# GpSimd's share of layer 0 and of the LayerNorms moved to VectorE and ScalarE or folded away, in a two-layer float32 encoder

## The chip, the cores and the metric

The kernel runs on one core of one Trainium2 chip. The metric is the device time of one execution in microseconds, as the median of three timed executions. Beside these stands one execution taken with the hardware profiler; all rows and durations in this text come from that one.

## The reference, cut to what matters

Two encoder layers over 256 tokens with 2048 features, all in float32. `cond` is silu(c); `g`, `sc` and `sh` are columns of the modulation.

```
for l in range(2):
    mod = cond @ w_ada[l] + b_ada[l]               # 6 parts: sh1, sc1, g1, sh2, sc2, g2
    u = x * (1.0 + sc1) + sh1
    proj = u @ w_in[l]                             # queries, keys, values of three groups of heads
    ... three attentions (4, 6 and 6 heads), each RMS-normalised -> y
    x = layer_norm(ALPHA * x + (1.0 + g1) * (y @ w_o[l]), ln1_g[l], ln1_b[l])
    u = x * (1.0 + sc2) + sh2
    gu = u @ w_gu[l]
    h = silu(gu[..., :5632]) * gu[..., 5632:]
    x = layer_norm(ALPHA * x + (1.0 + g2) * (h @ w_down[l]), ln2_g[l], ln2_b[l])
```

ALPHA is the square root of 2, and `layer_norm` divides by the root of the variance plus 1e-5.

## The kernel before, in words

**Layout.** Features lie on the 128 partitions, the 256 tokens on the free axis. A tile of 128 features by 256 tokens is one k of a product; a product of depth 2048 has 16 of them. The residual state is `ax`, 16 such tiles.

**Products.** TensorE multiplies in a reduced float32 form, so each operand is split into two halves that are exact in it: a weight piece `raw` (128x2048, 1 MB, one DMA on SP's queue) becomes `hi` on ScalarE (L246) and `lo` = raw - hi on VectorE (L247), each in two pieces of 1024 columns. An input tile X holds its high half in columns 0 to 255 and its low half in 256 to 511. For one 128x128 block of weights, a pair of matmuls runs: `hi` against all 512 columns (L262, or L538 in a stream), and `lo` against the first 256 (L263, L539). The accumulator has two halves that still have to be added: `combine` copies the second half on ScalarE (`cmb`, L279) and adds the first on VectorE (L282); `combine_add`, for a sum that is continued, uses ScalarE (L286), GpSimd (L287) and VectorE (L288). Only the last product of a run, `gemm_last` (L273), uses three matmuls of 256 columns for a block and one 256-column accumulator.

**Buffers.** `raw` and the modulation's weights `ada` share four buffers of 1 MB, in the order in which they are asked for on SP; `hi` and `lo` have four buffers each. A DMA therefore waits on SP until the fourth piece before it has been used up by VectorE.

**Modulation.** A column of 128 features is one VectorE pass over 128x2048 of `w_ada` (L200), 96 for a layer, followed by `ada_finish`, which adds the bias, and 1.0 for scales and gates (L190): in layer 0 once for each column. `first_x` makes the first 16 input tiles out of scale and shift (parts 1 and 0) as they arrive. The other columns are spread over the products by `pace` and `need`. DEFER = 6 columns of parts 4 and 3 are left for the first feed-forward.

**GpSimd.** It scales `ax` by ALPHA (L386), sums squares for the RMS norms (L328), adds in `combine_add` and in `residual` (L509, L518), and in `ln_and_next` computes coefficients (L461 to L463) and the new `ax` = ALPHA * (normalised * g + b) for every k (L493). In the head of a product that follows a LayerNorm it also makes the second `lo` piece of every weight tile but the first.

**Heads.** After a LayerNorm the next product starts with six tiles of n side by side, so that each X that arrives feeds six pairs. For each k VectorE makes `lt` from `ax` (L479, L480), ScalarE makes `lu` (L491) and the high half of X (L291), VectorE the low half of X (L292). There are three such heads: the first feed-forward (`gu0`, twelve tiles of which the first 11 k are summed while the last X arrive, results `gup`), the second layer's w_in (`in1`) and its feed-forward (`gu1`).

**Order.** Within an engine instructions run in the order in which a scheduler put them, with priorities from the order of the code; `ada` passes of the first two parts of layer 0 have high priority, all others low.

## Time and profile before

| | |
|---|---|
| three timed executions | 2382.51, 2383.88, 2376.82 us; median 2382.51 us |
| profiled execution, by its span | 2378.3 us, 4.2 us under the median of the timed ones |
| mean granted TensorE clock | 0.980 of full speed |
| busy: TensorE, VectorE, ScalarE, GpSimd | 94%, 76%, 50%, 19% of the span |
| moved by DMA | 590.62 MB, 248 GB/s on average |

The stages by time: 0 to 167 us first modulation columns and first part of w_in; 167 to 373.6 us attention of layer 0 with the rest of w_in; 373.6 to 460 us w_o of layer 0; to 466 us its LayerNorm; 466 to 554 us head of the first feed-forward (to the end of the sums over 11 k); to 1250 us the rest of it and the second LayerNorm; 1250 to 1302 us head of w_in of layer 1; to 1600 us its attention and w_o; 1600 to 1650 us LayerNorm and head of the second feed-forward; the rest to the end. The busy share of TensorE counts matmuls that wait inside for data, so lost time is read against the pitch of undisturbed matmuls and from waits, stage by stage.

### The profile page before, as it was taken

The numbers are of one execution on the slowest core, as the hardware profiler recorded it, in microseconds if no ns is written. First come the engines' busy times: TensorE is split into PE (matmuls) and PEld (weight loads), VectorE is DVE, ScalarE is ACT, GpSimd is POOL, SyncE is SP. The second block draws the span as 40 slices with busy tenths as digits, with TensorE's granted clock in tenths as the row PEclk, the third lists the DMA queues.
The fourth block names the chain that finished last, engine by engine and source line by source line (L and its number), as shares of the span: only waits on it lengthen the run. The fifth ranks groups of instructions, "written<-read, shape, count | busy, mean of one in ns | idle before, by whom it ended". The sixth has DMA issues, their size and how long they took to land.

```text
span 2378.3 us, 32888 instructions
## 1 busy us (share of the span) xinstructions
PE 2245.7 (94%) x12426; PEld 1926.3 (81%) x12426; DVE 1800.8 (76%) x2556; ACT 1195.4 (50%) x2028; POOL 460.4 (19%) x412
## 2 busy tenths in 40 slices
PE   5778999989999999999999999999999999999997
PEld 3667787777888888888877888887888888888886
DVE  7878998889888788898778575678666665556556
ACT  3345555454445444445446665646444444444445
POOL 1022235462000210020154000344000011011014
PEclk8889999999999999999999999999999999999999
DMA  9886886667899888889864454365667666546543
GB/s 371 326 305 235 318 315 260 230 256 280 293 332 342 278 326 331 295 321 335 295 231 174 156 211 177 140 232 181 220 217 270 232 203 235 182 160 213 189 157 109
DMA packets 88433, 590.62 MB, mean 248 GB/s; under 512 B 9937, under 2 KB 10065, under 8 KB 28881
## 3 DMA queue, kind: packets, MB, share of 16 engines
q1 hardware_dynamic: 88274, 588.52, 68.1%
q8 instruction: 97, 1.59, 0.3%
q14 instruction: 62, 0.51, 0.1%
HBM read 586.39 MB, written 2.10 MB: 247 GB/s over the span
## 4 chain that ended last, share of the span: by engine, by line
PE 72%; DVE 14%; ACT 4%; issue 4%; DMA 3%; POOL 2%; ACTq 0%; DVEq 0%; POOLq 0%; SPq 0%
PE gu L262 25%; PE gu L263 13%; PE dn L262 9%; DVE ada L200 6%; PE dn L263 4%; DVE lo L247 3%; DMA ada<-in_w_ada 3%; PE o L262 3%; PE in L262 3%; PE in L538 2%; ACT hi L246 2%; PE o L263 2%; PE in L263 1%; DVE X L292 1%; PE in L539 1%
## 5 line engine op out<-in xcount | busy, mean ns | idle before, releaser
L247 DVE TENSOR_TENSOR lo<-raw,hi 128x1024 fp32r<-128x1024 f32 (+2 forms) x787 | 896.8, 1150 | 373.7 <-ACT hi L246 368.8
L246 ACT ACTIVATE hi<-raw 128x1024 fp32r<-128x1024 f32 (+2 forms) x808 | 775.6, 969 | 636.0 <-PE gu L262 218.8
L262 PE MATMUL gu<-X,hi 128*128 128x512 f32 x2528 | 888.3, 396 | 1.3 <-ACT H L291 1.3
L263 PE MATMUL gu<-X,lo 128*128 128x256 f32 x2528 | 710.7, 281 | 4.5 <-DVE lo L247 4.5
L262 PEld LDWEIGHTS gu<-X,hi 128*128 128x128 f32 x2528 | 475.2, 188 | 113.5 <-ACT H L291 1.6
L262 PE MATMUL dn<-H,hi 128*128 128x512 f32 x1386 | 487.8, 397 | 0.0
L263 PEld LDWEIGHTS gu<-X,lo 128*128 128x128 f32 x2528 | 479.0, 189 | 5.4 <-DVE lo L247 5.4
L200 DVE CUSTOM_DVE_ANT_0 ada<-ada,cond 128x2048 f32<-128x2048 f32 x192 | 444.2, 2314 | 36.1 <-DMA ada<-in_w_ada 26.6
L263 PE MATMUL dn<-H,lo 128*128 128x256 f32 x1386 | 387.9, 281 | 5.9 <-DVE lo L247 5.8
L262 PEld LDWEIGHTS dn<-H,hi 128*128 128x128 f32 x1386 | 260.5, 188 | 62.9 <-DVE H L292 1.5
L263 PEld LDWEIGHTS dn<-H,lo 128*128 128x128 f32 x1386 | 261.7, 189 | 9.1 <-DVE lo L247 8.6
L538 PE MATMUL in<-X,hi 128*128 128x512 f32 x464 | 184.7, 437 | 55.6 <-DVE X L292 48.9
L287 POOL TENSOR_TENSOR mix<-mix,cma 128x256 f32<-128x256 f32 x64 | 77.5, 1211 | 670.6 <-ACT cma L286 665.9
L538 PEld LDWEIGHTS in<-X,hi 128*128 128x128 f32 x464 | 96.4, 209 | 85.6 <-DVE X L292 54.9
L539 PE MATMUL in<-X,lo 128*128 128x256 f32 x464 | 137.4, 306 | 5.9 <-DVE lo L247 5.8
L539 PEld LDWEIGHTS in<-X,lo 128*128 128x128 f32 x464 | 96.3, 210 | 9.8 <-DVE lo L247 8.4
L262 PE MATMUL in<-X,hi 128*128 128x512 f32 x272 | 97.1, 399 | 0.0
L838 ACT ACTIVATE gu<-gu 128x256 f32<-128x256 f32 x82 | 34.2, 417 | 89.0 <-DVE gu L282 88.8
L518 POOL TENSOR_TENSOR s<-s,ax 128x256 f32<-128x256 f32 x56 | 68.9, 1230 | 51.0 <-DVE ax L510 39.8
L461 POOL TENSOR_TENSOR cf<-vec,mod 128x1 f32<-128x1 f32 (+1 forms) x18 | 7.8, 433 | 366.4 <-DVE mod L190 366.2
L263 PE MATMUL in<-X,lo 128*128 128x256 f32 x272 | 77.8, 286 | 0.0
L279 ACT ACTIVATE cmb<-gu 128x256 f32<-128x256 f32 x164 | 60.3, 368 | 28.2 <-PE gu L263 26.5
(321 smaller groups left out, 2922.5 us busy)
## 6 DMA issues: line engine op xcount, KB each, us to landing
ada<-in_w_ada SPq DMA_DIRECT2D x192, 1024.0 KB, 5.6
raw<-in_w_gu SPq DMA_DIRECT2D x176, 1024.0 KB, 4.9
raw<-in_w_dn SPq DMA_DIRECT2D x128, 704.0 KB, 4.2
raw<-in_w_in SPq DMA_DIRECT2D x46, 1024.0 KB, 4.8
raw<-in_w_o SPq DMA_DIRECT2D x32, 1024.0 KB, 5.0
raw<-in_w_va SPq DMA_DIRECT2D x8, 1024.0 KB, 4.9
raw<-in_w_uq SPq DMA_DIRECT2D x6, 1024.0 KB, 4.8
raw<-in_w_vc SPq DMA_DIRECT2D x4, 1024.0 KB, 5.7
```

What stands on the lines that cost most here:

```text
L200: ve.tensor_tensor_reduce(out=w, in0=w, in1=cond, op0=ALU.mult, op1=ALU.add, scale=1.0, scalar=0.0, accum_out=mods[l, part][:, k:k + 1])
L246: ac.activation(out=hi[:, :n], in_=raw[:, c0:c0 + n], func=AF.Copy)
L247: eng.tensor_tensor(out=lo[:, :n], in0=raw[:, c0:c0 + n], in1=hi[:, :n].bitcast(F32), op=ALU.subtract)
L262: pe.matmul(acc[:], lhsT=h, rhs=X[k][:], start=(i == 0), stop=False)
L263: last_mm[0] = raw_ins(pe.matmul(acc[:, :S], lhsT=lo, rhs=X[k][:, :S], start=False, stop=(i == len(kts) - 1)))
L279: ac.activation(out=t, in_=acc[:, S:], func=AF.Copy, scale=scale)
L287: po.tensor_tensor(out=dst, in0=dst, in1=t, op=ALU.add)
L292: return ve.tensor_tensor(out=dst[:, S:], in0=u, in1=dst[:, :S].bitcast(F32), op=ALU.subtract)
L518: (ve if n == KT - 1 else po).tensor_tensor(out=s1, in0=s1, in1=ax[:, n], op=ALU.add)
L538: pe.matmul(acc[:], lhsT=h, rhs=X[k][:], start=first, stop=False)
L539: last_mm[0] = raw_ins(pe.matmul(acc[:, :S], lhsT=lo, rhs=X[k][:, :S], start=False, stop=end))
L838: ac.activation(out=hs[0], in_=hs[0], func=AF.Silu)
```

## The change

The state `ax` is kept as x instead of ALPHA * x: the gates (parts 2 and 5) are divided by ALPHA and the LayerNorm's 1e-5 by ALPHA squared, so that L386 goes. VectorE writes `lt` into `ax`, and g * lt + b is done there later by ScalarE (`affine`). The bias enters the modulation's pass as its initial value; only scales (part 1, 4) get + 1 on ScalarE, and gates (1 + g) / ALPHA on VectorE, in layer 0 in groups of four columns (part 1: one). In layer 0 the products with w_in, kn, qn, qp, w_o and the first twelve tiles of the feed-forward's first 11 k take three matmuls of 256 columns in a 256-column accumulator (860 blocks of 128x128 in place of pairs, counted by line in the order of after, of them 240 in w_o and 192 in the head), and `take` (one ScalarE copy) or `take_add` (one VectorE op) ends them. GpSimd's coefficients, sums of squares, second `lo` pieces and layer 0's adds for s1 go to VectorE. DEFER goes from 6 to 8.

```diff
-DEFER = 6
+DEFER = 8
-    ve.memset(eps_ln, LN_EPS)
+    ve.memset(eps_ln, LN_EPS / (ALPHA * ALPHA))
     def ada_finish(l, part, c0, n):
         m = mods[l, part][:, c0:c0 + n]
-        b = vcol(l, V_ADA + part * KT + c0, n)
-        plus = 0.0 if part in (0, 3) else 1.0
-        ve.scalar_tensor_tensor(out=m, in0=m, scalar=plus, in1=b, op0=ALU.add, op1=ALU.add)
+        if part in (2, 5):
+            ve.tensor_scalar(out=m, in0=m, scalar1=1.0, scalar2=1.0 / ALPHA, op0=ALU.add, op1=ALU.mult)
+        elif part in (1, 4):
+            ac.activation(out=m, in_=m, func=AF.Copy, bias=1.0)
...
-                                        scalar=0.0, accum_out=mods[l, part][:, k:k + 1])
-            if l == 0:
-                ada_finish(l, part, k, 1)
-            elif k == KT - 1:
-                ada_finish(l, part, 0, KT)
+                                        scalar=vcol(l, V_ADA + part * KT + k), accum_out=mods[l, part][:, k:k + 1])
+            g = ada_group(l, part)
+            if k % g == g - 1:
+                ada_finish(l, part, k + 1 - g, g)
...
+    def mm_one(acc, h, lo, x, first, end):
+        pe.matmul(acc[:, :S], lhsT=h, rhs=x[:, :S], start=first, stop=False)
+        pe.matmul(acc[:, :S], lhsT=h, rhs=x[:, S:], start=False, stop=False)
+        last_mm[0] = raw_ins(pe.matmul(acc[:, :S], lhsT=lo, rhs=x[:, :S], start=False, stop=end))
+
+    def take(acc, dst, scale=1.0):
+        ac.activation(out=dst, in_=acc[:, :S], func=AF.Copy, scale=scale)
+
+    def take_add(acc, dst, scale=1.0):
+        ve.scalar_tensor_tensor(out=dst, in0=acc[:, :S], scalar=scale, in1=dst, op0=ALU.mult, op1=ALU.add)
...
-            po.tensor_tensor(out=acc_tile, in0=acc_tile, in1=t, op=ALU.add)
+            ve.tensor_tensor(out=acc_tile, in0=acc_tile, in1=t, op=ALU.add)
...
-        po.tensor_scalar(out=ax[:, k], in0=ax[:, k], scalar1=ALPHA, scalar2=None, op0=ALU.mult)
...
         def coef(k0, n):
-            po.tensor_tensor(out=a_, in0=lg[:, k0:k0 + n], in1=sc_[:, k0:k0 + n], op=ALU.mult)
+            ve.tensor_tensor(out=a_, in0=lg[:, k0:k0 + n], in1=sc_[:, k0:k0 + n], op=ALU.mult)
...
         def make(k):
-            if by_k:
+            if by_k and k % 4 == 0:
                 need(l, 4, k)
                 need(l, 3, k)
-                coef(k, 1)
+                coef(k, 4)
             t = tmp(f"lt{l}_{which}_{k}")
             ve.tensor_tensor(out=t, in0=ax[:, k], in1=bcr[:, :S], op=ALU.mult)
-            ve.tensor_tensor(out=t, in0=t, in1=bcn[:, :S], op=ALU.add)
+            t, t_ = ax[:, k], t
+            ve.tensor_tensor(out=t, in0=t_, in1=bcn[:, :S], op=ALU.add)
...
-            po.tensor_scalar(out=ax[:, k], in0=t, scalar1=cf[:, 2, k:k + 1], scalar2=cf[:, 3, k:k + 1],
-                             op0=ALU.mult, op1=ALU.add)
+            later.append((k, l, gb))
...
+    def affine(n):
+        for _ in range(min(n, len(later))):
+            k, l_, gb = later.pop(0)
+            ac.activation(out=ax[:, k], in_=ax[:, k], func=AF.Identity, scale=vcol(l_, gb + k),
+                          bias=vcol(l_, gb + KT + k))
...
-        if final and n == KT - 1:
+        if final and (n == KT - 1 or one):
...
-                (ve if n == KT - 1 else po).tensor_tensor(out=s1, in0=s1, in1=ax[:, n], op=ALU.add)
+                (ve if n == KT - 1 or one else po).tensor_tensor(out=s1, in0=s1, in1=ax[:, n], op=ALU.add)
...
-                self.cur = wload(self.src[i // KT], 2048, (1024, 1024), g_, (ve, po) if self.gates and i else None)
+                self.cur = wload(self.src[i // KT], 2048, (1024, 1024), g_)
...
-            if n == KT - 1:
+            if n == KT - 1 or l == 0:
                 gemm_last(acc, get, Y, allk)
...
-                combine(accs[n] if n < HB else st_gu.tile(n, 0, KS), parts[n])
+                take(accs[n] if n < HB else st_gu.tile(n, 0, KS), parts[n])
```

`affine(2)` is called at each later tile of w_in of layer 1 and each later feed-forward pair, `affine(16)` before w_o. Where these and the rest come to stand is set by the scheduler; three places follow.

VectorE in the head of the first feed-forward, from the low half of X 7 on (X_1_7; `lt` are the normalised tiles, `lo` the low halves of weights, `ada` a modulation column). Before:

```order
L292 TENSOR_TENSOR X_1_7_4021<-lu_1_7_4020,X_1_7_4021 128x256
L480 TENSOR_TENSOR lt_1_9_4075<-lt_1_9_4075,lnbn_1_3790 128x256
L292 TENSOR_TENSOR X_1_8_4055<-lu_1_8_4054,X_1_8_4055 128x256
L479 TENSOR_TENSOR lt_1_10_4099<-ax,lnbr_1_3789 128x256
L247 TENSOR_TENSOR lo_0_4119<-raw_4116,hi_0_4118 128x1024
L292 TENSOR_TENSOR X_1_9_4079<-lu_1_9_4078,X_1_9_4079 128x256
L480 TENSOR_TENSOR lt_1_10_4099<-lt_1_10_4099,lnbn_1_3790 128x256
L200 ISA ada_4_13_4279,mod_4_101<-ada_4_13_4279,cond 128x2048
L200 ISA mod_4_101 128x1
L292 TENSOR_TENSOR X_1_10_4103<-lu_1_10_4102,X_1_10_4103 128x256
```

Now, to the same two steps further:

```order
L205 ISA ada_3_12_4681,mod_3_100<-ada_3_12_4681,cond,vec 128x2048
L205 ISA mod_3_100 128x1
L315 TENSOR_TENSOR X_1_7_4456<-lu_1_7_4455,X_1_7_4456 128x256
L253 TENSOR_TENSOR lo_1_4485<-raw_4478,hi_1_4484 128x1024
L500 TENSOR_TENSOR lt_1_8_4491<-ax,lnbr_1_4209 128x256
L253 TENSOR_TENSOR lo_0_4566<-raw_4563,hi_0_4565 128x1024
L502 TENSOR_TENSOR ax<-lt_1_8_4491,lnbn_1_4210 128x256
L500 TENSOR_TENSOR lt_1_9_4517<-ax,lnbr_1_4209 128x256
L253 TENSOR_TENSOR lo_1_4570<-raw_4563,hi_1_4569 128x1024
L315 TENSOR_TENSOR X_1_8_4495<-lu_1_8_4494,X_1_8_4495 128x256
L502 TENSOR_TENSOR ax<-lt_1_9_4517,lnbn_1_4210 128x256
L205 ISA ada_4_13_4684,mod_4_101<-ada_4_13_4684,cond,vec 128x2048
```

Both `lo` pieces of a tile now stand on VectorE, and three modulation passes (before: one) stand ahead of X 10.

SP's queue at the same place, from the first weights of w_gu whose loads follow those of w_o. Before:

```order
L238 DMA raw_4116<-in_w_gu 128x2048
L238 DMA raw_4201<-in_w_gu 128x2048
L238 DMA raw_4260<-in_w_gu 128x2048
L198 DMA ada_4_13_4279<-in_w_ada 128x2048
L198 DMA ada_3_13_4283<-in_w_ada 128x2048
L198 DMA ada_4_14_4326<-in_w_ada 128x2048
L198 DMA ada_3_14_4330<-in_w_ada 128x2048
L238 DMA raw_4352<-in_w_gu 128x2048
L198 DMA ada_4_15_4383<-in_w_ada 128x2048
L198 DMA ada_3_15_4387<-in_w_ada 128x2048
L238 DMA raw_4419<-in_w_gu 128x2048
```

Now:

```order
L244 DMA raw_4646<-in_w_gu 128x2048
L203 DMA ada_3_12_4681<-in_w_ada 128x2048
L203 DMA ada_4_13_4684<-in_w_ada 128x2048
L203 DMA ada_3_13_4687<-in_w_ada 128x2048
L203 DMA ada_4_14_4690<-in_w_ada 128x2048
L203 DMA ada_3_14_4693<-in_w_ada 128x2048
L203 DMA ada_4_15_4696<-in_w_ada 128x2048
L203 DMA ada_3_15_4700<-in_w_ada 128x2048
L244 DMA raw_4740<-in_w_gu 128x2048
L244 DMA raw_4820<-in_w_gu 128x2048
```

Seven modulation loads now follow the sixth weight tile in one row; before, six followed the seventh, in two groups.

ScalarE in the head of w_in of layer 1, from `lu` 11 on (`hi` are high halves of weights, `cmb` the copy after the first of the six tiles). Before:

```order
L491 ACTIVATE lu_2_11_11526<-lt_2_11_11523,cf_2_11211 128x256
L291 ACTIVATE X_2_11_11527<-lu_2_11_11526 128x256
L246 ACTIVATE hi_0_11598<-raw_11596 128x1024
L491 ACTIVATE lu_2_12_11547<-lt_2_12_11544,cf_2_11211 128x256
L291 ACTIVATE X_2_12_11548<-lu_2_12_11547 128x256
L246 ACTIVATE hi_1_11602<-raw_11596 128x1024
L491 ACTIVATE lu_2_13_11558<-lt_2_13_11555,cf_2_11211 128x256
L291 ACTIVATE X_2_13_11559<-lu_2_13_11558 128x256
```

Now:

```order
L513 ACTIVATE lu_2_11_12012<-ax,cf_2_11710 128x256
L314 ACTIVATE X_2_11_12013<-lu_2_11_12012 128x256
L530 ACTIVATE ax<-ax,vec 128x256
L252 ACTIVATE hi_1_12083<-raw_12077 128x1024
L513 ACTIVATE lu_2_12_12032<-ax,cf_2_11710 128x256
L314 ACTIVATE X_2_12_12033<-lu_2_12_12032 128x256
L530 ACTIVATE ax<-ax,vec 128x256
L252 ACTIVATE hi_0_12139<-raw_12137 128x1024
L513 ACTIVATE lu_2_13_12042<-ax,cf_2_11710 128x256
L314 ACTIVATE X_2_13_12043<-lu_2_13_12042 128x256
L530 ACTIVATE ax<-ax,vec 128x256
```

The scheduler puts the 16 `affine` operations (L530) between the head's own steps, about one after each X.

## Rows read from the trace of the kernel before

**Rows 1.** The page: busy time by engine, and the chain that ended last, by engine.
```profile
PE 2245.7 (94%) x12426; PEld 1926.3 (81%) x12426; DVE 1800.8 (76%) x2556; ACT 1195.4 (50%) x2028; POOL 460.4 (19%) x412
...
PE 72%; DVE 14%; ACT 4%; issue 4%; DMA 3%; POOL 2%; ACTq 0%; DVEq 0%; POOLq 0%; SPq 0%
```

**Rows 2.** Stretches: length, busy PE, PEld, DVE, ACT, POOL (count), granted clock, DMA share, GB/s.
```profile
0.00:167.00 167.00, 109.70 (x441) 85.39 (x442) 128.65 (x179) 59.06 (x96) 27.33 (x32) 0.86 0.87 336
167.00:373.60 206.60, 190.04 (x1030) 160.11 (x1028) 187.93 (x343) 118.05 (x255) 60.59 (x61) 0.97 0.79 291
373.60:460.00 86.40, 80.52 (x454) 69.10 (x455) 75.97 (x93) 39.86 (x63) 48.07 (x41) 0.98 0.73 266
...
466.00:554.00 88.00, 75.15 (x386) 61.24 (x384) 80.79 (x113) 47.43 (x84) 60.89 (x46) 0.96 0.61 230
1250.00:1302.00 52.00, 47.26 (x262) 39.77 (x261) 44.45 (x68) 33.46 (x54) 24.17 (x21) 1.00 0.49 175
1600.00:1650.00 50.00, 45.19 (x243) 37.09 (x242) 45.11 (x79) 35.42 (x62) 24.58 (x21) 1.00 0.43 151
...
20.00:60.00 40.00, 23.08 (x89) 18.75 (x88) 34.99 (x46) 10.67 (x17) 9.13 (x6) 0.77 0.98 383
```

**Rows 3.** Waits: 0 to 167 us, w_o, heads in1 and gu1; total, times, longest.
```profile
PE in L538 <- DVE X L292: 44.1, 10, 8.6
...
PE o L263 <- DVE lo L247: 5.1, 6, 2.0
...
PE in L538 <- DVE X L292: 4.7, 4, 1.7
...
PE gu_h L538 <- DVE X L292: 4.5, 4, 1.7
```

**Rows 4.** TensorE: timeline at head in1 (start, length), chain at w_o's last tile, weight loads.
```profile
1250.83 0.40 PE L538 MATMUL in<-X,hi 128*128 128x512 f32 x1
...
1251.88 0.39 PE L538 MATMUL in<-X,hi 128*128 128x512 f32 x1
...
454.06 5.76 PE o L273 x48
...
L262 PEld LDWEIGHTS gu<-X,hi 128*128 128x128 f32 x2528 | 475.2, 188 | 113.5 <-ACT H L291 1.6
```

**Rows 5.** Groups on VectorE, 0 to 167 us: busy us, mean ns; idle before.
```profile
L200 DVE CUSTOM_DVE_ANT_0 ada<-ada,cond 128x2048 f32<-128x2048 f32 x33 | 75.3, 2284 | 9.1 <-ACT cond L160 9.1
L190 DVE SCALAR_TENSOR_TENSOR mod<-mod,vec 128x1 f32<-128x1 f32 x33 | 4.9, 155 | 0.6
```

**Rows 6.** The same for 167 to 373.6 us.
```profile
L247 DVE TENSOR_TENSOR lo<-raw,hi 128x1024 fp32r<-128x1024 f32 (+1 forms) x47 | 57.7, 1244 | 3.8 <-ACT hi L246 3.6
...
L282 DVE SCALAR_TENSOR_TENSOR qc<-in,cmb 128x256 f32<-128x256 f32 x6 | 2.5, 419 | 0.3 <-ACT cmb L279 0.3
```

**Rows 7.** The same for w_o of layer 0.
```profile
L519 DVE TENSOR_TENSOR s<-s,rq_o 128x256 f32<-128x256 f32 x14 | 12.4, 886 | 1.5 <-ACT rq_o L517 1.5
```

**Rows 8.** The same for head gu0, 466 to 554 us.
```profile
L200 DVE CUSTOM_DVE_ANT_0 ada<-ada,cond 128x2048 f32<-128x2048 f32 x9 | 22.9, 2540 | 1.7 <-DMA ada<-in_w_ada 1.7
L247 DVE TENSOR_TENSOR lo<-raw,hi 128x1024 fp32r<-128x1024 f32 x11 | 17.9, 1626 | 0.0
L292 DVE TENSOR_TENSOR X<-lu,X 128x256 fp32r<-128x256 f32 x14 | 12.2, 870 | 1.2 <-ACT X L291 1.1
L839 DVE TENSOR_TENSOR gup<-gup,gup 128x256 f32<-128x256 f32 x4 | 6.4, 1606 | 0.0
```

**Rows 9.** Head gu0: first `lt` (chain) and X 10's low half (VectorE's timeline): start, length.
```profile
464.30 0.43 DVE lt L479
...
493.71 0.41 DVE L292 TENSOR_TENSOR X<-lu,X 128x256 fp32r<-128x256 f32 x1
```

**Rows 10.** Groups of the whole run: `lo` on VectorE, and ScalarE's affine at the end.
```profile
L247 DVE TENSOR_TENSOR lo<-raw,hi 128x1024 fp32r<-128x1024 f32 (+2 forms) x787 | 896.8, 1150 | 373.7 <-ACT hi L246 368.8 <-ACT ysqa L327 0.6
...
L450 ACT ACTIVATE ax<-lt,vec 128x256 f32<-128x256 f32 x16 | 8.1, 589 | 1.4 <-POOL lt L446 1.2
```

More of the change, by code (lines that the diff above doesn't have):

```diff
@@ L537, in mm @@
             self.pos += 1
+            if self.one:
+                mm_one(acc, h, lo, X[k], first, end)
+                return
             pe.matmul(acc[:], lhsT=h, rhs=X[k][:], start=first, stop=False)
@@ L562, in head_block @@
         return accs
-    st_in = Stream(_stream0(), w_in[0], "in0")
+    st_in = Stream(_stream0(), w_in[0], "in0", one=True)
     for l in range(L):
@@ L570, in w_in_tile @@
                 if n in EARLY:
[L571 removed]
+                    take_add(st_in.tile(n, HK, KT), dst, scale)
                 else:
[L573 removed]
+                    take(st_in.tile(n, 0, KT), dst, scale)
                 return
             get = wload(w_in[l, n], 2048, (1024, 1024))
+            affine(2)
             acc = pg(f"in{l}_{n}")
@@ L634, in tile_encoder @@
                 n = EARLY[j]
-                combine(st_in.tile(n, 0, HK), early[n])
+                take(st_in.tile(n, 0, HK), early[n])
                 if j == 2:
```

58 lines of the change are left out of this document (35 added, 23 removed).

## The prediction

> **What bounds the kernel now.** I read the page first: busy time by engine and the chain that ended last [rows 1]. TensorE is busy 94% of the span and has 72% of the chain, VectorE 14% of it and GpSimd only 2%. So time that is merely taken off GpSimd is worth little; what it may be worth is what VectorE gets or has to give, where TensorE waits for VectorE. Then the table by stretch [rows 2]: from 0 to 167 us TensorE is busy 110 of 167 us and VectorE 129; from 167 to 373.6 us VectorE is busy 188 of 206.6 us, in w_o of layer 0 76 of 86.4, in the head of the first feed-forward (gu0) 81 of 88, in the heads of w_in of layer 1 (in1) and of the second feed-forward (gu1) 44 of 52 and 45 of 50. Everywhere else TensorE runs nearly without a break, and the change has little to win. The waits tell whom TensorE waits for: X from VectorE for 44 us in the first stretch, `lo` for 5.1 in w_o, X for 4.7 and 4.5 in in1 and gu1 [rows 3].
>
> The price of TensorE's work is its pitch: three pairs of matmuls start between 1250.83 and 1251.88 us, 0.35 us each [rows 4]. The 192 pairs of gu0's head are then worth 67.2 us, where the stretch has 88.
>
> **The change part by part, against the span of 2378.3 us.**
>
> *TensorE.* The last tile of w_o already uses three matmuls of 256 columns: 48 in 5.76 us, 0.12 each, 0.36 for a block [rows 4]. That is 10 ns over a pair, and for the 860 blocks of layer 0 8.6 us. In w_o it is 240 x 0.01 = 2.4 us on the path, in gu0's head 1.9; the other 4.3 lie where TensorE waits for VectorE anyway and are hidden, and if that cover goes they appear. The Trainium skill (TensorE: Matmul & The Clock Gate, Back-to-back issue gap) gives 262 cycles for 256 columns and 518 for 512, by which a block would cost 2.5 ns more and 860 blocks 2.2 us. The sum goes by the row.
>
> *0 to 167 us.* VectorE loses 33 bias steps of 0.155 us, 5.1 us [rows 5]. They stand in the same queue as the passes and the X that TensorE waits for, so they count. It loses 17 sums at the end of products (q, k and the first halves of w_in) at 0.42 [rows 6], 7.1 us, of which perhaps half is followed by something late. The bias step of the scales moves to ScalarE (16 of 128x1), in front of the step that makes u; ScalarE is busy 59 of 167 us and covers it. GpSimd's scalings by ALPHA go for nothing, as nothing waits for them. What is late next is the transfer: between 20 and 60 us the DMA share is 0.98 at 383 GB/s [rows 2]. If that is the end of what the queue gives, the gain is 0; if all passes, 5.1 + 7.1 + about 1 of stretched operations, 13. I take -8, since SP's loads themselves wait for VectorE to free the four buffers, which then happens sooner.
>
> *167 to 373.6 us.* Off VectorE: 24 sums of 0.42 (kn, qn, qp, qc), 10.0 us; 33 bias steps of 0.155, 5.1; and stretching: 47 `lo` take 1244 ns on average [rows 6] against 1150 in the whole run [rows 10], 4.4 us, part of which stays, since GpSimd keeps some work; I count 3. On VectorE: 17 sums of squares from GpSimd at 0.42, 7.1 us, and eight gate steps at 0.155, 1.2. Net -9.8, and as the bias steps there are stretched too, -10 to -11. VectorE is busy 91% here, so most passes: -9, between -3 (only where TensorE waits for it now) and -16 (all of the removed work, the sums of squares beside other waits).
>
> *w_o of layer 0.* VectorE's s2 additions take 886 ns instead of 0.42 beside GpSimd's adds [rows 7]: 14 x 0.47 = 6.5 us go; eight bias steps (1.2) and, through DEFER, one pass of 2.3 go. 14 s1 additions of 0.42 come, 5.9. Net -4.1. ScalarE's and GpSimd's step before the residual goes too, off the path. TensorE's 5.1 us of waits for `lo` [rows 3] and the loss at the start shrink, against +2.4 of pitch: -3.5, between -7 and +2.4.
>
> *Head gu0.* Stretched operations return to their plain length when GpSimd falls silent [rows 8]: 9 passes 2.54 to 2.28, 2.3 us; 11 `lo` 1.63 to 1.15, 5.2; 14 X 0.87 to 0.42, 6.3; 4 products 1.61 to 0.42, 4.8. With 12 sums of 0.42 (5.0) and eight bias steps (1.2) 24.8 us go. 11 second `lo` pieces at 1.15 come, 12.7; 12 small coefficient steps, not in the trace as such, at the 0.155 of the nearest row, 1.9; one more pass, 2.3: 16.9. Net -7.9, so 81 becomes 73, against TensorE's 69.1. But the order is worse at the start. From the first `lt` to the low half of X 10, VectorE has in the new order 24 steps on `lt` (0.41), 11 X (0.42), nine `lo` (1.15) and three passes (2.28): 9.8 + 4.6 + 10.4 + 6.8 = 31.6 us, so that X 10 ends at 464.3 + 31.6 = 495.9 if nothing waits, against 494.1 now [rows 9]: +2 for the first 66 blocks. Queued behind the three passes are X 7 to X 10, and so TensorE; a pass waits for its load, and this for the buffer four loads before. Behind X 10 the saving remains: about -8. I take -6, between +12 (each of four passes comes 2.5 us late) and -12.
>
> *Heads in1 and gu1.* Excess on VectorE goes (14 X at 0.45, 6.3 us, in each), five second `lo` (5.8) come: about even. ScalarE gets 16 affine steps at 0.589 [rows 10], 9.4 us in 52 and 50: 33.5 becomes 42.9 and 35.4 becomes 44.8 [rows 2]. They stand between `lu` and X, and the last three X come behind one more `hi`. On the other side the `lo` from GpSimd, 2.4 us long before, is in time. +1 for each head, between -1.5 and +4.4 (four of these steps and two `hi` of about 1.0 in front of one X).
>
> *The rest.* Layer 1's attention has its sums of squares on VectorE with idle time to spare, the state's affine leaves the LayerNorms' GpSimd, the feed-forward's own sums are as before: -1, between -2 and 0.
>
> Sum: -8 - 9 - 3.5 - 6 + 1 + 1 - 1 = -25.5, span 2352.8. The median of the timed runs is 4.2 above the span: **2357 us**.
>
> **The rivals.**
>
> *The start does not move.* Transfers set the pace to 167 us, and in the attention the sums of squares stand in front of the scores that TensorE needs: 0 and -3 instead of -8 and -9. For it speaks the DMA share, against it that 0.98 holds for 40 us and 0.87 for the stretch. Time: 2357 + 14 = 2371.
>
> *All of VectorE's saving passes.* -13, -15, -7, -10, 0, 0, -1: -46, 2336. For it speaks that VectorE is the bound of these stretches; against it that ScalarE's `hi` and the loads follow closely behind.
>
> *The heads lose.* VectorE's and ScalarE's in-order queues delay X at their high ends: +12, +4.4 and +4.4 in place of -4, with the rest as forecast: 2357 + 25 = 2382, no change. Decided if the passes come late in gu0; in the trace of before only one of them waited for its load, 1.7 us in all [rows 8].
>
> *Slower: a weight load in front of each matmul.* A pair has two loads, a block now three, each 188 ns as shown [rows 4], in layer 0. If they were not hidden, a block would cost 3 x 0.188 = 0.564 us, 0.21 over the pair; for the 432 blocks on the path (w_o, gu0's head) +92 instead of +4.3, and the kernel would take about 2445. It becomes slower from 25.5 us more in 432 blocks, 0.42 us for a block. The row of w_o's last tile, with 0.36, speaks against it. The Trainium skill (TensorE: Matmul & The Clock Gate, The mechanism, Part 3) says that a load overlaps running matmuls only when its row group differs; here all use the whole array, and the pitch of 0.35 with two loads of 188 ns shows overlap nevertheless.
>
> **How the numbers follow.** Forecast 2357: 0.58. The start does not move, 2371: 0.14. All passes, 2336: 0.12. Heads lose, 2382: 0.10. Weight loads or another order of the same size, slower: 0.06. A difference under 0.3%, 7 us, can hardly be told from none. Faster than 2375 are the first three, 0.84, less 0.03 for a forecast that misses by its whole width: 0.81; same 0.12; slower 0.07. The range reaches from the case in which all passes to just under that in which the heads lose: 2334 to 2378, leaving out about 0.2.
>
> **What would show it.** Right if VectorE's passes in the first 100 us stand closer by some 0.7 us for each four; if 167 to 373.6 us shrinks by about 9; if w_o's s2 additions take 0.42 and its blocks 0.36; if X 10 of gu0 ends about 31.6 us after the first `lt`, and the head of 192 blocks lasts about 82 us; if in1's waits for X stay near 5. Wrong if blocks cost more than 0.36, if the first DMA-bound stretch keeps its length, or if TensorE waits over 4 us for an X behind a pass or an affine step.

## The result, and the profile after

The changed kernel takes 2343.2 us (median of four executions, 2333.95 to 2353.45) against 2381.8 for the kernel before: a ratio of 0.986, 95% interval 0.982 to 0.990. The forecast was 2357. The profiled execution has a span of 2351.7 us (forecast 2352.8) and was the longest of the four, so the stages below are those of a long one; of the shorter ones there is no trace.

The page of after, busy time and chain (before: [rows 1]):

```profile
PE 2244.0 (95%) x13286; PEld 1973.5 (84%) x13286; DVE 1763.9 (75%) x2498; ACT 1209.2 (51%) x2054; POOL 200.5 (9%) x175
...
PE 69%; issue 18%; DVE 7%; ACT 3%; POOL 1%; DMA 1%; ACTq 0%; POOLq 0%; DVEq 0%; SPq 0%
```

GpSimd lost 260 us of work, VectorE 37, ScalarE gained 14; what the kernel gained is 27 us of span. VectorE's share of the chain was halved, from 14% to 7%. The 18% of "issue" are no trait of the kernel: in its second profile (again) they are 3%, with TensorE at 83% and VectorE at 8%. The table by stretch, with the columns of [rows 2] and the same pieces of work:

```profile
0.00:156.90 156.90, 109.67 (x638) 97.77 (x639) 120.88 (x135) 63.41 (x112) 2.52 (x6) 0.89 0.93 359
156.90:355.30 198.40, 187.92 (x1305) 174.74 (x1303) 179.77 (x310) 113.58 (x240) 8.09 (x6) 0.97 0.83 309
355.30:435.70 80.40, 79.38 (x650) 79.38 (x650) 65.49 (x96) 35.17 (x49) 0.00 (x0) 0.98 0.72 256
442.00:520.60 78.60, 72.28 (x579) 71.16 (x578) 74.93 (x115) 55.07 (x96) 0.00 (x0) 0.98 0.77 283
577.00:1219.00 642.00, 624.20 (x3533) 540.28 (x3532) 527.13 (x640) 302.45 (x473) 71.66 (x59) 1.00 0.84 302
1232.00:1282.00 50.00, 46.69 (x258) 39.25 (x258) 40.42 (x71) 39.65 (x70) 0.00 (x0) 1.00 0.48 168
1581.00:1620.00 39.00, 35.62 (x195) 29.63 (x195) 32.57 (x63) 34.40 (x63) 0.00 (x0) 1.00 0.40 137
```

Stage lengths in us, from TensorE's timeline at marks of equal work, for before, after and three of the experiments below. (The attention ends where its last sum of squares is spread to all partitions; a few blocks of w_o run before that, and how many differs a little, so it is best read together with w_o.)

| stage | before | after | change | forecast | bias | pairs | lo_first |
|---|---|---|---|---|---|---|---|
| to 192 blocks of w_in | 167.1 | 156.9 | -10.2 | -8 | 166.4 | 163.7 | 159.0 |
| attention, layer 0 | 206.4 | 198.4 | -8.0 | -9 | 204.5 | 197.0 | 199.0 |
| w_o, layer 0, and LayerNorm | 92.9 | 86.9 | -6.0 | -3.5 | 91.3 | 94.0 | 87.9 |
| head gu0, first 66 blocks | 31.0 | 32.6 | +1.6 | +2 | 31.1 | 29.8 | 31.6 |
| head gu0, next 126 blocks | 55.4 | 45.9 | -9.5 | -8 | 54.7 | 51.8 | 46.7 |
| to the first dn product | 60.7 | 56.4 | -4.3 | 0 | 58.4 | 58.6 | 56.4 |
| feed-forward of layer 0 to LayerNorm | 624.7 | 642.1 | +17.4 | 0 | 628.4 | 630.9 | 625.0 |
| LayerNorm and head in1 | 64.0 | 62.8 | -1.2 | +1 | 64.0 | 61.6 | 61.5 |
| attention and w_o, layer 1 | 297.4 | 292.5 | -4.9 | -1 | 295.5 | 292.4 | 292.3 |
| LayerNorm and head gu1 | 47.0 | 45.5 | -1.5 | +1 | 46.9 | 45.5 | 45.6 |
| the rest | 731.7 | 731.8 | 0 | 0 | 731.8 | 726.5 | 731.8 |

To the first dn product (dn is the product with w_down, which the feed-forward of a layer runs in four parts) the change is worth 36.4 us, 10 more than forecast; the feed-forward of layer 0, whose instructions the change barely touches, gives 17.4 back in this profile.

### The profile page after: what moved, and what is told of

The parts are those of the page before. It is cut to its first block, busy times and chain, and to the rows that moved or that the text cites. A ratio compares the mean times of both kernels' runs of the same rounds, so it can differ in the third digit from the quotient of the medians.

```text
span 2351.7 us, 34259 instructions
## 1 busy us (share of the span) xinstructions
PE 2244.0 (95%) x13286; PEld 1973.5 (84%) x13286; DVE 1763.9 (75%) x2498; ACT 1209.2 (51%) x2054; POOL 200.5 (9%) x175
## 4 chain that ended last, share of the span: by engine, by line
PE 69%; issue 18%; DVE 7%; ACT 3%; POOL 1%; DMA 1%; ACTq 0%; POOLq 0%; DVEq 0%; SPq 0%
PE gu L268 18%; PE gu L269 9%; PE dn L268 8%; PE dn L269 4%; PE o L279 4%; DVE ada L205 3%; PE in L268 3%; DVE lo L253 2%; PE o L268 2%; ACT hi L252 2%; PE in L269 1%; PE in L289 1%; PE in L291 1%; PE in L290 1%; PE o L269 1%
## 5 line engine op out<-in xcount | busy, mean ns | idle before, releaser
L205 DVE CUSTOM_DVE_ANT_0 ada<-ada,cond,vec 128x2048 f32<-128x2048 f32 x192 | 449.7, 2350 | 55.8 <-DMA ada<-in_w_ada 46.5
L310 POOL TENSOR_TENSOR mix<-mix,cma 128x256 f32<-128x256 f32 x64 | 78.5, 1227 | 1185.5 <-ACT cma L309 1176.9
L289 PE MATMUL in<-X,hi 128*128 128x256 f32 x368 | 106.2, 313 | 41.9 <-ACT X L314 35.3
L289 PEld LDWEIGHTS in<-X,hi 128*128 128x128 f32 x368 | 73.3, 212 | 47.2 <-ACT X L314 39.1
L290 PE MATMUL in<-X,hi 128*128 128x256 f32 x368 | 110.2, 303 | 1.5 <-DVE X L315 1.5
L291 PE MATMUL in<-X,lo 128*128 128x256 f32 x368 | 107.6, 302 | 1.8 <-DVE lo L253 1.8
L268 PE MATMUL in<-X,hi 128*128 128x512 f32 x272 | 97.0, 398 | 0.0
L880 ACT ACTIVATE gu<-gu 128x256 f32<-128x256 f32 x82 | 34.2, 418 | 94.3 <-DVE gu L305 94.3
L290 PEld LDWEIGHTS in<-X,hi 128*128 128x128 f32 x368 | 76.9, 209 | 2.7 <-DVE X L315 2.1
L291 PEld LDWEIGHTS in<-X,lo 128*128 128x128 f32 x368 | 75.4, 208 | 3.0 <-DVE lo L253 2.6
L269 PE MATMUL in<-X,lo 128*128 128x256 f32 x272 | 77.9, 286 | 0.0
L305 DVE SCALAR_TENSOR_TENSOR gu<-gu,cmb 128x256 f32<-128x256 f32 x158 | 65.9, 417 | 3.3 <-ACT cmb L302 3.2
```

The lines of the kernel that those rows point to most:

```text
L205: ve.tensor_tensor_reduce(out=w, in0=w, in1=cond, op0=ALU.mult, op1=ALU.add, scale=1.0, scalar=vcol(l, V_ADA + part * KT + k), accum_out=m ...
L268: pe.matmul(acc[:], lhsT=h, rhs=X[k][:], start=(i == 0), stop=False)
L269: last_mm[0] = raw_ins(pe.matmul(acc[:, :S], lhsT=lo, rhs=X[k][:, :S], start=False, stop=(i == len(kts) - 1)))
L289: pe.matmul(acc[:, :S], lhsT=h, rhs=x[:, :S], start=first, stop=False)
L290: pe.matmul(acc[:, :S], lhsT=h, rhs=x[:, S:], start=False, stop=False)
L291: last_mm[0] = raw_ins(pe.matmul(acc[:, :S], lhsT=lo, rhs=x[:, :S], start=False, stop=end))
```

## The experiments

**The changed kernel once more** ("again"), with nothing edited.

> The changed kernel once more, nothing edited. In its first profile layer 0's feed-forward (first dn product to the LayerNorm) took 642.1 us, 17.4 more than before, and that execution was the longest of four (2353 us, the others 2334 to 2346). Theory A, the new order is the cause: one modulation pass now stands a `lo` piece further ahead on VectorE in each dn product, waits there for its load, and delays `lo`; then this profile shows the same loss, the feed-forward at 638 to 645 us. Theory B, it differs from execution to execution (transfers that come a little later at a DMA share of 0.86): then the stage may take anything from 624 to 642 us, and the total goes with it, 2334 to 2353. Both expect the other stages within 1 us of the first profile: 192 blocks of w_in at 157, attention 198, w_o 80, 192 blocks of the first head 78.5.

Measured: 2342.6 us, ratio 0.986 (0.984 to 0.989). All stages are within 0.2 us of the first profile up to the first dn product; the feed-forward took 639.7, a loss of 15.0 against before. This profile too was taken of the longest of its four executions (2351 against 2341 to 2344). How far the loss is one of the order and how far one of the execution is taken up at lo_first, with the profiles of the other runs.

**Layer 0 in pairs again** ("pairs").

```diff
-    st_in = Stream(_stream0(), w_in[0], "in0", one=True)
+    st_in = Stream(_stream0(), w_in[0], "in0")
...
-                take(acc, d_, sc_)
+                combine(acc, d_, sc_)
...
-            if n == KT - 1 or l == 0:
+            if n == KT - 1:
                 gemm_last(acc, get, Y, allk)
...
```

> The changed kernel with layer 0's products as pairs again (two halves of the accumulator, the copy and the sums on ScalarE, VectorE and GpSimd, w_o's residual with its GpSimd steps). If the sums taken off VectorE are what shortened layer 0, then the first 192 blocks of w_in take about 160 us instead of 157 (17 sums back), the attention 203 instead of 198 (24 sums, 10 us of work, half on the path), w_o 83 instead of 80 (GpSimd's adds stretch s2), the head of 192 blocks 80 instead of 78.5; total +10 to +13 over the changed kernel. Rival, the pitch: pairs are 10 ns shorter, 8.6 us for 860 blocks; if that weighs more than the sums, layer 0 gets shorter, by up to 6 us.

Measured: 2357.3 us, ratio 0.992 (0.989 to 0.994). Without the one accumulator the first stretch takes 163.7 us (6.8 of its 10.2 back), w_o 87.3 instead of 80.4, the head's 192 blocks 81.6 instead of 78.5, but the attention 197.0, no longer than with it. The single accumulator, with the shorter ends of products and the residual that go with it, is half of the gain to the first dn product: 18.0 of 36.4 us. The rival, the shorter pitch of pairs, would have made layer 0 shorter; of these stages the attention is, by 1.4 us, and the start of the head (29.8 us for 66 blocks, with one pass less ahead of X 10).

**The same steps on VectorE, the accumulator kept** ("take_ve").

```diff
     def take(acc, dst, scale=1.0):
-        ac.activation(out=dst, in_=acc[:, :S], func=AF.Copy, scale=scale)
+        ve.tensor_scalar(out=dst, in0=acc[:, :S], scalar1=scale, scalar2=None, op0=ALU.mult)
```

> The changed kernel with the single copy that ends a one-accumulator product on VectorE instead of ScalarE: 53 steps of about 0.4 us return to VectorE in layer 0, with the accumulators, GpSimd and ScalarE's other work as changed. If the sums that left VectorE are what shortened the first stretch (theory of the prediction), 192 blocks of w_in come at about 161 to 163 us and the attention takes 201 to 203 us instead of 198; the head of 192 blocks 80 to 82 instead of 78.5. If it was the shorter chain behind a product (one step in place of two or three) and GpSimd's silence, the first stretch stays within 1.5 us of 157 and the attention within 1 of 198.

Measured: 2346.4 us, ratio 0.986 (0.982 to 0.989). The first stretch goes from 156.9 to 161.7 us, so 4.8 of the 6.8 are the steps on VectorE (to be read with a scatter of some 3 us in that stretch, of which at accsq_pool). The attention takes 197.3 and w_o 79.2: there the 24 steps cost nothing on VectorE. The head of 192 blocks takes 79.7 instead of 78.5.

**The other half of X first** ("xlow_first"): the rival that TensorE gains because a block's first matmul needs only the half of X that ScalarE writes.

```diff
-        pe.matmul(acc[:, :S], lhsT=h, rhs=x[:, :S], start=first, stop=False)
-        pe.matmul(acc[:, :S], lhsT=h, rhs=x[:, S:], start=False, stop=False)
+        pe.matmul(acc[:, :S], lhsT=h, rhs=x[:, S:], start=first, stop=False)
+        pe.matmul(acc[:, :S], lhsT=h, rhs=x[:, :S], start=False, stop=False)
```

> The changed kernel, but the first of the three matmuls of a block takes the low half of X, so that it waits for VectorE's step as the pairs' 512-column matmul did; nothing else moves. If part of the gain is that TensorE may begin a block on the high half, which ScalarE has ready earlier, then 192 blocks of w_in come at about 159 to 161 us instead of 157, and the first head's 66 blocks take 33.5 to 35 us instead of 32.6. If the gain lies in the sums that left VectorE, both stay within 0.7 us.

Measured: 2345.7 us, ratio 0.987 (0.985 to 0.989); the first stretch 154.8, the first 66 blocks 29.9, and the next 126 50.9 instead of 45.9, 2.6 of it one wait for weights. In the first stretch the rival falls: waiting for the later half did not make it longer. In the head the run can't tell: with the edit the scheduler also put two passes and eight `lo` pieces on VectorE ahead of X 10, instead of three and nine, which is 3.6 us less, and the first 66 blocks are 2.7 us shorter; the head as a whole takes 80.8 instead of 78.5.

**The bias alone** ("bias"): the kernel before, with this edit and no other.

```diff
-        b = vcol(l, V_ADA + part * KT + c0, n)
-        plus = 0.0 if part in (0, 3) else 1.0
-        ve.scalar_tensor_tensor(out=m, in0=m, scalar=plus, in1=b, op0=ALU.add, op1=ALU.add)
+        if part in (2, 5):
+            ve.tensor_scalar(out=m, in0=m, scalar1=1.0, scalar2=1.0, op0=ALU.add, op1=ALU.mult)
+        elif part in (1, 4):
+            ac.activation(out=m, in_=m, func=AF.Copy, bias=1.0)
...
-                                        scalar=0.0, accum_out=mods[l, part][:, k:k + 1])
+                                        scalar=vcol(l, V_ADA + part * KT + k), accum_out=mods[l, part][:, k:k + 1])
```

> The kernel before with one part of the change alone: the bias enters the modulation's pass, scales get + 1 on ScalarE, gates + 1 on VectorE, column by column in layer 0; no bias step for shifts. If the bias steps in VectorE's queue are what the first stretch pays for (theory A), 192 blocks of w_in come at about 160 us instead of 167 (33 passes, 5.1 us of steps and what they stretch) and the attention takes 203 instead of 206.4; total -8 to -11 against before. Theory B, the first stretch was shortened by the sums that left VectorE (with pairs put back it lost 6.8 of 10.2 us): then only about 3 us are gained there and 1 to 3 in the attention, total -4.

Measured: 2377.6 us, ratio 0.999 (0.998 to 1.001): no change. The first stretch gains 0.7 us. Two rows say why. The first is the group of modulation passes on VectorE to 166.4 us (busy, mean ns), to be read against [rows 5]; the second is the stretch of 20 to 60 us, against the last line of [rows 2]:

```profile
L201 DVE CUSTOM_DVE_ANT_0 ada<-ada,cond,vec 128x2048 f32<-128x2048 f32 x33 | 76.6, 2345 | 9.4 <-ACT cond L160 9.4
```

```profile
20.00:60.00 40.00, 23.52 (x92) 19.27 (x91) 34.91 (x35) 12.65 (x24) 9.14 (x6) 0.76 0.96 382
```

A pass that starts from the bias takes 2345 ns instead of 2284, so 0.06 of the 0.155 us comes back at once; and from 20 to 60 us the transfers run at 382 GB/s, as before (383). By TensorE's timeline the run is 1.6 us ahead of before at the 96th of the 192 blocks (90.6 against 92.2 us) and 0.7 at the last. Theory B is the nearer one, and its 3 us for the stretch were still too many.

**Sums of squares back on GpSimd** ("accsq_pool").

```diff
-            ve.tensor_tensor(out=acc_tile, in0=acc_tile, in1=t, op=ALU.add)
+            po.tensor_tensor(out=acc_tile, in0=acc_tile, in1=t, op=ALU.add)
```

> The changed kernel with the sums of squares back on GpSimd (34 additions in both layers). By the prediction's sum 17 additions of 0.42 us in layer 0's attention weigh 7.1 us on VectorE, most of it on the path: attention 198.4 goes to about 193. Rival: GpSimd's additions stretch VectorE's passes and `lo`, and this costs as much: 198 to 200 us. Layer 1's attention, where VectorE has idle time: 214.9 unchanged within 1 by the first, up to 3.5 longer (218.4 before) by the second.

Measured: 2345.8 us, ratio 0.987 (0.984 to 0.989); attention of layer 0 198.9 instead of 198.4, of layer 1 218.5 instead of 214.9. The 7.1 us that the sum had laid on VectorE's path in layer 0 aren't there, and in layer 1 the move is worth 3.6 us. Part of that is TensorE's wait for these sums at the end of a group: 3.5 us in five waits with GpSimd, 1.6 in one with VectorE. Where the other 1.7 come from isn't shown. (The first stretch, 159.3, differs by 2.4 although nothing in it was edited and the traces have the same sequence of operations on TensorE, VectorE and ScalarE there. VectorE's passes wait 2.1 us for their loads before 70 us, where none of after is listed as waiting for one. Runs with that sequence take 156.0 to 159.3 us, so 3 us in that stretch tell nothing of an edit.)

**GpSimd's `lo` pieces in the heads again** ("lo_pool").

```diff
-                self.cur = wload(self.src[i // KT], 2048, (1024, 1024), g_)
+                self.cur = wload(self.src[i // KT], 2048, (1024, 1024), g_, (ve, po) if self.gates and i else None)
```

> The changed kernel with the second `lo` piece of each weight tile of the three heads back on GpSimd (21 pieces). If contention of GpSimd with VectorE is what made the heads long, X steps and passes are stretched again (X 0.8 us instead of 0.42) and the head of 192 blocks goes from 78.5 to 83 or 86 us, the heads of w_in and of the second feed-forward from 50 and 39 to 51 and 40. Rival, VectorE's queue is the limit: 11 pieces of 1.15 us come off it in the first head, and it gets shorter, to 74 us.

Measured: 2360.1 us, ratio 0.993 (0.991 to 0.995). The head's 192 blocks take 88.1 us instead of 78.5, in1 52.1 instead of 50.1, gu1 39.4 instead of 38.8. GpSimd's and VectorE's timelines (start, length) in the first head, then two groups there, against [rows 8]:

```profile
451.18 2.40 POOL L253 TENSOR_TENSOR lo<-raw,hi 128x1024 fp32r<-128x1024 f32 x1 [4.55 <-ACT hi L252]
...
467.78 2.49 POOL L253 TENSOR_TENSOR lo<-raw,hi 128x1024 fp32r<-128x1024 f32 x1 [7.08 <-ACT hi L252]
```

```profile
452.57 1.29 DVE L315 TENSOR_TENSOR X<-lu,X 128x256 fp32r<-128x256 f32 x1 [0.84 <-ACT X L314]
...
468.04 2.50 DVE L315 TENSOR_TENSOR X<-lu,X 128x256 fp32r<-128x256 f32 x1
```

```profile
L205 DVE CUSTOM_DVE_ANT_0 ada<-ada,cond,vec 128x2048 f32<-128x2048 f32 x10 | 29.4, 2940 | 1.5 <-DMA ada<-in_w_ada 1.5
...
L315 DVE TENSOR_TENSOR X<-lu,X 128x256 fp32r<-128x256 f32 x14 | 10.2, 737 | 2.8 <-ACT X L314 2.8
```

GpSimd's pieces end at 453.58 and 470.27, the X steps that began beside them at 453.86 and 470.54: 0.28 and 0.27 later, whatever they had begun with. A step of 0.42 us is not slowed but held until GpSimd is done. The Trainium skill (SBUF — State Buffer, Who interferes with whom) says that a VectorE instruction with two SBUF inputs is blocked by a GpSimd one that reads SBUF, for the whole instruction, if that was first; the two pairs of rows agree to 0.3 us. Without GpSimd, X takes 420 ns and a pass 2343 (rows of after below).

**DEFER at 6** ("defer6").

```diff
-DEFER = 8
+DEFER = 6
```

> The changed kernel with DEFER = 6 as before. If the passes that stand ahead of X 7 to X 10 cost the start of the first head (the forecast has +2 us for its first 66 blocks), these take 31 instead of 32.6 us, w_o gets 1 to 2.3 us longer for the pass that returns to it: total within 2 us of the changed kernel. If the passes wait for their loads there (the forecast's high end), the first 66 blocks fall to 28 or 29 us and the total falls by 2 to 4.

Measured: 2354.6 us, ratio 0.990 (0.988 to 0.993). The first 66 blocks take 27.4 us instead of 32.6, so the passes cost the start of the head 5.2 us, but w_o takes 93.4 instead of 80.4. In w_o VectorE now has 13 passes instead of 6, and TensorE waits there once for weights, 9.6 us:

```profile
L205 DVE CUSTOM_DVE_ANT_0 ada<-ada,cond,vec 128x2048 f32<-128x2048 f32 x13 | 30.4, 2344 | 0.0
```

With columns finished in groups of four, `need` rounds the column asked for up to the end of its group; at 6 it is the last one, and nothing is deferred. So DEFER and the groups belong together, and I had priced DEFER's move at one pass.

**The affine behind the head** ("affine_late").

```diff
         for _ in range(min(n, len(later))):
             k, l_, gb = later.pop(0)
-            ac.activation(out=ax[:, k], in_=ax[:, k], func=AF.Identity, scale=vcol(l_, gb + k),
-                          bias=vcol(l_, gb + KT + k))
+            with after(xact[1]):        # the last X of the head on ScalarE
+                ac.activation(out=ax[:, k], in_=ax[:, k], func=AF.Identity, scale=vcol(l_, gb + k),
+                              bias=vcol(l_, gb + KT + k))
```

> The changed kernel with ScalarE's affine operations ordered behind the last X of their head. If they delay X in the heads (+1 us was forecast for each of the heads of w_in and of the second feed-forward, at most 4.4), these heads fall from 50.1 and 38.8 us to 49 and 38 or less; if ScalarE has room for them, both stay within 0.3 us. The first head: 32.6 for 66 blocks to 31 or less by the first, unchanged by the second.

Measured: 2341.1 us, ratio 0.985 (0.982 to 0.988). in1 49.8 (50.1 and 49.4 in the two profiles of after), gu1 38.8: no difference, ScalarE has room. The first head takes 28.0 us for 66 blocks instead of 32.6, but 52.2 instead of 45.9 for the next 126. That the affine stood in the way there isn't shown: with the edit the scheduler also put two passes and seven `lo` pieces on VectorE ahead of X 10, instead of three and nine, 4.8 us less. In the next 126 blocks TensorE waits once, and long, for weights (wait, total, times, longest); in after, no wait of TensorE is listed for those blocks:

```profile
PE gu L289 <- ACT hi L252: 4.3, 1, 4.3
```

**`lo` before the pass** ("lo_first"), the disputed feed-forward of layer 0.

```diff
-            with after(gate[0]), tc.high_priority(100 if l == 0 and part < 2 else -1000):
-                ve.tensor_tensor_reduce(...)
...
...
+            if hold[0]:                       # in layer 0's feed-forward
+                held.append((l, part, k, w))
+            else:
+                ada_pass(l, part, k, w)
...
+        while held:                           # at the end of wload
+            ada_pass(*held.pop(0), behind=raw_ins(lo_i))
```

> The changed kernel, but in layer 0's feed-forward each modulation pass is ordered behind the `lo` pieces of the weight tile before which its load was issued, so that a late load of a pass delays no `lo` of that tile. Theory A (the order costs 17 us): the feed-forward falls from 642 to about 625 us and TensorE's waits for `lo` there from 16 to under 5 us. Theory B (executions differ): it stays between 624 and 642 as in the unedited kernel. A loss is possible if buffers come free later: SP's waits for VectorE grow and the stage goes above 642.

Measured: 2335.3 us, ratio 0.982 (0.979 to 0.984), on the same chip as "again" with 2342.6. The feed-forward falls to 625.0 us. The waits on either side of it, first of after, then of lo_first:

```profile
PE dn L269 <- DVE lo L253: 11.6, 10, 1.6
PE gu L269 <- DVE lo L253: 4.8, 2, 2.7
...
DVE ada L205 <- DMA ada<-in_w_ada: 42.8, 22, 4.1
```

```profile
PE dn L282 <- DVE lo L264: 5.9, 8, 1.2
PE gu L282 <- DVE lo L264: 1.1, 1, 1.1
```

The same stage of the kernel before, and of pairs, which has after's order there:

```profile
PE dn L263 <- DVE lo L247: 5.8, 7, 1.1
PE gu L263 <- DVE lo L247: 3.5, 2, 2.2
...
DVE ada L200 <- DMA ada<-in_w_ada: 22.5, 18, 3.2
```

```profile
PE dn L269 <- DVE lo L253: 5.6, 8, 1.9
PE gu L269 <- DVE lo L253: 1.6, 1, 1.6
...
DVE ada L205 <- DMA ada<-in_w_ada: 24.3, 17, 3.1
```

In after a pass that waits for its load holds back the `lo` behind it, and TensorE waits for that, 17.6 us in all with the waits for H. What both theories had wrong is where the order differs: not in each dn product, but only in the first of the four, where a pass stood between the two `lo` pieces of a weight tile and now stands ahead of both; in the other three they stand nearly as before. On VectorE, before and after:

```profile
631.93 0.96 DVE L247 TENSOR_TENSOR lo<-raw,hi 128x768 fp32r<-128x768 f32 x1 [1.03 <-ACT hi L246]
633.79 2.29 DVE L200 CUSTOM_DVE_ANT_0 ada<-ada,cond 128x2048 f32<-128x2048 f32 x1 [0.90 <-DMA ada<-in_w_ada]
...
636.35 0.81 DVE L247 TENSOR_TENSOR lo<-raw,hi 128x640 fp32r<-128x640 f32 x1
```

```profile
597.06 2.35 DVE L205 CUSTOM_DVE_ANT_0 ada<-ada,cond,vec 128x2048 f32<-128x2048 f32 x1 [2.42 <-DMA ada<-in_w_ada]
...
599.34 0.95 DVE L253 TENSOR_TENSOR lo<-raw,hi 128x768 fp32r<-128x768 f32 x1
```

TensorE's longest wait in after's stage, on VectorE and on TensorE:

```profile
641.46 2.35 DVE L205 CUSTOM_DVE_ANT_0 ada<-ada,cond,vec 128x2048 f32<-128x2048 f32 x1 [4.07 <-DMA ada<-in_w_ada]
643.73 0.08 DVE L205 DVE_READ_ACCUMULATOR2_ANT mod<- 128x1 f32 x1
643.73 1.22 DVE L253 TENSOR_TENSOR lo<-raw,hi 128x1024 fp32r<-128x1024 f32 x1
```

```profile
645.01 0.39 PE L269 MATMUL gu<-X,lo 128*128 128x256 f32 x1 [2.67 <-DVE lo L253]
```

With `lo` first no wait of VectorE for a modulation load is listed in that stretch.

How much of the loss is the order can't be read from after and again alone. Seven more runs have after's order in this stage, and their profiles give it 631 to 640 us, with 7.9 to 16.7 us of TensorE's waits for `lo` and H: take_ve 640.5 us, lo_pool 639.1, defer6 636.8, xlow_first 634.8, accsq_pool 634.1, affine_late 632.3, pairs 631.1. So the same order loses 6 to 17 us against before (624.7), by how late the loads come: VectorE's passes wait 24 to 43 us for them, before 22.5. Theory A holds in that a pass ahead of `lo` can cost TensorE time, and that `lo` first takes most of it away: the three runs with it have 624 to 625 us and 2.4 to 7.0 us of waits, and lo_first's four executions (2328 to 2339 us) all lie below those of again (2341 to 2351), 7.3 us by the medians. Theory B holds in that the size differs from execution to execution: TensorE's waits go with those of the passes, from 7.9 us beside 24.3 (pairs) to 17.6 beside 42.8 (after). In bias too the passes of the first dn product stand ahead of both pieces; they wait 13.8 us in the stage, and TensorE 7.2.

**Thinner loads** ("rate", "rate2"), both with `lo` first.

```diff
-RATE = ((0.19, 0.135, 0.135), (0.04, 0.05, 0.05))
+RATE = ((0.19, 0.11, 0.11), (0.08, 0.08, 0.08))       # rate
+RATE = ((0.19, 0.125, 0.125), (0.10, 0.05, 0.05))     # rate2
```

> The kernel of the run with `lo` first, and the modulation's loads spread thinner over layer 0's feed-forward: 15 of 75 columns of layer 1 are loaded in layer 1 instead. If the DMA queue with a share of 0.86 is what leaves TensorE waiting there, the feed-forward falls from 625 to 619 to 622 us (the rest of its waits, 9 us, shrinks), with layer 1's attention and w_o within 1.5 us: total 2330 or less. If the waits have another cause, it stays at 623 to 628 and layer 1 pays 0 to 3 us.

> The kernel of the run with `lo` first, with the modulation's loads thinner in layer 0's feed-forward and denser in layer 1's attention (7 columns move from the one to the other, and the loads before the last columns of w_o of layer 1 don't come in a burst: in the run before, 12 or more of them in w_o made it 97.4 us instead of 77.6). If the loads' share of the DMA queue is what is left of the feed-forward's waits (9 us with `lo` first, 3 with 15 columns less), the feed-forward's waits fall to about 6 us and layer 1's attention and w_o take at most 3 us more: total 2328 to 2335, within the scatter of the kernel with `lo` first. If layer 1's w_o has no room for two or three more passes on VectorE, it grows to 82 or more and the gain is lost: 2336 to 2342.

Measured: rate 2354.8 us, ratio 0.990 (0.987 to 0.992); rate2 2333.8 us, ratio 0.981 (0.979 to 0.984). In rate TensorE's listed waits in the feed-forward fell from 7.0 to 2.4 us, of a single kind, so thinner loads do take them away. That the stage still took 624.1 us is TensorE's pitch, which was mostly the longer of two there (see the last section):

```profile
PE dn L282 <- DVE lo L264: 2.4, 2, 1.2
```

But w_o of layer 1 took 97.4 us instead of 77.6, since the columns that layer 1 then still lacked were all asked for at one of its tiles. In rate2 the feed-forward took 623.7, w_o of layer 1 78.7 and its attention 216.5. rate2 is faster than both kernels; against lo_first (2335.3) it can't be told apart.

## Why the prediction was right, and where not

**The total.** The range held the time. With 2343.2 it lies between the forecast, 2357, and the case in which all of VectorE's saving passes, 2336. The span came within 1.1 us of the forecast, but by luck, through errors of opposite sign: -36.4 instead of -26.5 to the first dn product, then +17.4 instead of 0, then -7.6 instead of +1.

**0 to 167 us (-8, measured -10.2).** The size was near, the step was not. The bias steps, 5.1 us "in the same queue as the passes", were worth 0.7 by themselves (bias). I had read the DMA share of 0.98 as a bound that would give way because SP waits for VectorE. From 20 to 60 us it hardly does (0.98 at 383 GB/s before, 0.97 at 381 in after); from 60 to 100 us it does (0.88 at 339, then 0.96 at 366). The passes do stand closer, by 0.64 us for each four to 100 us, as the prediction's sign had it: VectorE's 21st pass starts at 94.3 us before, 93.0 in bias and 91.5 in after. But TensorE's 96th block comes only 3.3 us sooner than before (88.9 against 92.2), and the other 6.9 of the 10.2 us come behind it. Nor was the pass's new operand free, 0.06 us each. The 17 sums at the ends of products, which I halved to 3.5, carry the stretch: 6.8 with their accumulator (pairs), 4.8 by VectorE's share alone (take_ve). TensorE's granted clock, 0.86 before and 0.89 after, does not explain the gain: again has 0.87 and the same 156.9 us. The rival "the start does not move" was right for the rate of 20 to 60 us and wrong for the rest.

**Attention of layer 0 (-9, measured -8.0).** The size was right, its parts were not. The 24 sums off VectorE, 10 us in my sum, are worth nothing there (take_ve -1.1, pairs -1.4 against after), and the 7.1 us of sums of squares cost nothing (accsq_pool +0.5). The bias is 1.9 of the 8. VectorE's busy 91% was no sign that it sets the pace. What the other 6 come from was not separated: pairs, which has all but the accumulator, has them.

**w_o of layer 0 (-3.5, measured -5.7 without the LayerNorm).** Right in kind, and larger. The pitch is as read, 8 matmuls in 0.96 us:

```profile
434.88 0.96 PE o L279 x8
```

and TensorE is now the bound, 79.4 of 80.4 us; of waits only 1.0 us is left. s2 takes its plain length, and s1 comes beside it, as the working had it:

```profile
L548 DVE TENSOR_TENSOR s<-s,ax 128x256 f32<-128x256 f32 x14 | 5.9, 421 | 0.2
L549 DVE TENSOR_TENSOR s<-s,rq_o 128x256 f32<-128x256 f32 x14 | 5.9, 418 | 0.0
```

Pairs (87.3 us, with DEFER at 8 and the bias as in after) shows that it is the accumulator, which takes ScalarE and GpSimd out of the residual; the bias alone made w_o and the LayerNorm 1.6 us shorter.

**Head gu0 (+2, then -8; measured +1.6, then -9.5).** Right in its steps. X 10 was to end 31.6 us after the first `lt`; it does so 31.45 after (440.30 to 471.75), with the three passes in front of it. Part of the agreement is luck: the steps follow one another a little before the one ahead has ended, so that VectorE is busy for 29.8 us of it and idle for 1.7, mostly waiting for ScalarE. In after's timeline of VectorE:

```profile
440.30 0.42 DVE L500 TENSOR_TENSOR lt<-ax,lnbr 128x256 f32<-128x256 f32 x1 [0.79 <-PE lnbr L451]
...
467.53 2.34 DVE L205 CUSTOM_DVE_ANT_0 ada<-ada,cond,vec 128x2048 f32<-128x2048 f32 x1
...
471.33 0.42 DVE L315 TENSOR_TENSOR X<-lu,X 128x256 fp32r<-128x256 f32 x1
```

The steps went back to their plain lengths, to be read against [rows 8]:

```profile
L205 DVE CUSTOM_DVE_ANT_0 ada<-ada,cond,vec 128x2048 f32<-128x2048 f32 x10 | 23.4, 2343 | 0.0
...
L315 DVE TENSOR_TENSOR X<-lu,X 128x256 fp32r<-128x256 f32 x14 | 5.9, 420 | 1.1 <-ACT X L314 1.1
```

lo_pool puts a price on the contention: +9.6 us for the head, the lower granted clock of its first 66 blocks included (0.86 instead of 0.97). What I didn't count are the products behind the head (-4.3 to the first dn). That gain is not the contention, since lo_pool has 56.4 us there as well; pairs has 58.6 and bias 58.4 where before has 60.7 with 2.3 us of listed waits and a granted clock of 0.97 instead of 1.00. How it divides stays open.

**Feed-forward of layer 0 (0, measured +17.4).** The step that failed, though the total held. I took it "as before" because its instructions are the same, and looked neither at their order nor at how late the loads of the passes come. The in-order wait that I had priced for the head, a pass that waits for its load in front of a step that TensorE needs, is at work here too, before as after. Of the 17.4 about 10 are waits: what TensorE's matmuls start late by adds up to some 12 us before and 23 in after (the listed waits for `lo` and H alone are 9.3 and 17.6). About 6 are the pitch, of which below. In the other profiles with after's order the late starts are 12 to 22 us, in bias 10 and in lo_first 10. So the order lets late loads cost TensorE time, but how much more than before they cost by it isn't settled, with one profile of before. Of the nine profiles with after's order, after (642.1) and again (639.7), from which the loss was first read, lie at the long end.

**Layer 1 (+1, measured -7.6).** The heads lost nothing to the affine (affine_late), so +1 for each should have been a small gain from GpSimd's silence (lo_pool: 2.0 and 0.6). TensorE's waits for X in in1 were to stay near 5 us and are 3.3. The sums of squares are worth 3.6 in the attention, where I had counted 1.

**Slower by weight loads** is refuted by w_o's 0.12 us for a matmul, each with a load of its own.

**What stays open.** The median lies 14 us under the forecast although the span met it: I had put the median 4.2 us above the profiled span, and it lies 8.5 below, because the profiled executions of after and again were the longest of their four. That the others lose less in the feed-forward fits the seven profiles with the same order, which lose 6 to 16 us there, but of the others themselves there is no trace. The span of before lay among its times.
